# Eight loads for the edge rows and a new order at the start of a pooling and ConvFFN layer

## Chip, cores and metric

The kernel runs on one core of one Trainium2 chip (trn2). The metric is device time in microseconds (us) of one execution. The engines are called PE (TensorE; PEld is its weight load), ACT (ScalarE), DVE (VectorE), POOL (GpSimd) and SP (SyncE, which here only issues transfers).

## What is computed

One decoder layer in float32, x of 1024 positions by 1024 features: a norm, a causal pooling over windows of 2, 4, 8 and 16 positions (each for a quarter of the features) minus the position itself, a 256 x 256 product per quarter, a residual; then a second norm and a gated ConvFFN with 2816 hidden features.

```python
h = rms_norm(x, norm_mix_g)
# per group: mean of the last w positions of h, minus h; product with pool_w; bias; scale
x = x + pool_scale * (einsum('bsgc,gcd->bsgd', d, pool_w) + pool_b)
f = rms_norm(x, norm_ffn_g)
h = causal_depthwise_conv(f @ ffn_w_in, ffn_conv_w, ffn_conv_b)    # 3 taps
val, gate = split(h, 2)
out = x + (silu(gate) * val) @ ffn_w_out
```

## The kernel before

The layer has two parts. The large one (from 59 us on) is the ConvFFN: both products run on PE as seven-product block schemes (`step`, L384, and the output loop up to L723) over float32 operands split in a high and a low half. The change does not touch it. The small one, the mixer, runs over eight tiles of 128 positions, and the change is in the order of its first three tiles (L457 to L488) and in what is loaded ahead of them (L90 to L146).

For tile j the mixer works so. `load_x` (L85) brings x of the tile into SBUF. `stat(j)` (L453) squares and sums it on ACT (`rstd_of`, L155), takes the root there and three small steps on DVE, which give the factor of the norm. `mixer_norm(j)` (L174) multiplies a constant band matrix by that factor on DVE (`bandr`), so that the norm and the pooling are one product: `mixer_window(j)` (L234) multiplies x by the band on PE into a PSUM tile `psd`, adds the rows of the tile before (the edges) on DVE and copies the result to `dh` on ACT. `mixer_out(j)` (L254) multiplies `dh` by the pooling weights `wps` into `psy`, adds the bias rows by a product with ones (L262), adds x on DVE (L265) and stores the sum to DRAM (L266). `mixer_out_stats`, `ffn_norm` and `ffn_operand` then do the second norm and transpose the tile for the ConvFFN.

Ahead of that, things are made once: the weights `wps` (L205, eight DVE steps: pool_w times the pooling scale spread over partitions by `scale_rows`, times the norm's gain per partition from `par_sb`); the bias rows (`pool_bias`, L214, in two halves, loaded SBUF to SBUF into `bias_hl`); the second norm's factors spread over the partitions (`gain_spread` and `gain_rows`); and the edges: the last 16 positions of all eight tiles in one tile `x_edge` (L142), squared and normed as a tile of its own (`edge_norm`, L171) and multiplied by an edge band (`mixer_edges`, L187). `first_edges` (L246) adds the edges to tile 1's `dh`, which `mixer_window(1)` has already copied.

The order on each engine is written out: `with tc.issue_after(marks[...])` holds an instruction's place in the program behind a marked one, and each engine works strictly in its order. PE also has idle products (`keep_warm`, L127), whose result nobody reads. SP issues the loads in the order in which they are written. Every transfer of SP or ACT takes the next of eight semaphores in turn, and before a semaphore is taken again its last transfer must have landed.

## Time and profile before

| what | us |
|---|---|
| median of the runs | 703.62 |
| lowest run | 703.33 |
| profiled execution, its own time | 702.61 |
| span of its instructions | 700.9 |
| PE busy | 693.9 |
| DVE busy | 600.5 |
| ACT busy | 343.2 |
| POOL busy | 12.5 |

The profile is that of one execution. The span goes from the first to the last instruction; the execution's own time has 1.7 us more around it. Matmuls overlap in PE, so a row's length there is from the start of the first to the end of the last, and the next row can start before. On ACT and DVE too the next instruction may start some 0.1 us before the one before it ends.

### The profile page before, as it was taken

To read this page: it belongs to the slowest core of one execution; us is meant where nothing else is said; L and a number is where in the kernel's file an instruction comes from. 1 tells how busy PE (TensorE), PEld (TensorE's weight loads), DVE (VectorE), ACT (ScalarE), POOL (GpSimd) and SP (SyncE) were. 2 spreads that over 40 slices of the span, in tenths; PEclk is the share of its full clock that TensorE was granted. 3 is DMA by queue.
4 is the path that set the end of the run, shared out by engine and by line. 5 is a ranking of instruction groups with operands and counts; after the bars stand their busy time and mean duration, and the time that the engine had idled before them with its cause. 6 is when DMAs were issued, how large, how long until landed. Compare 5 with 4: busy or idle time off the path is not lost.

```text
span 700.9 us, 8493 instructions
## 1 busy us (share of the span) xinstructions
PE 693.9 (99%) x3154; PEld 573.7 (82%) x3154; DVE 600.5 (86%) x885; ACT 343.2 (49%) x515; POOL 12.5 (2%) x30
## 2 busy tenths in 40 slices
PE   8999999999999999999999999999999999999998
PEld 5898778888888888888888888888888888888886
DVE  5688999999888888888988888876887988999985
ACT  4786545454444444444545454454554444444431
POOL 3110000000000000000000000000000000000000
PEclk9999999999999999999999999999999999999999
DMA  9854112232222112222222212229989700122131
GB/s 307 302 141 121 57 65 91 89 122 91 67 84 74 60 78 90 91 90 91 91 90 91 86 65 91 91 84 338 335 305 335 277 22 1 61 90 87 64 106 60
DMA packets 32555, 85.47 MB, mean 122 GB/s; under 512 B 3689, under 2 KB 5377, under 8 KB 29698
## 3 DMA queue, kind: packets, MB, share of 16 engines
q1 hardware_dynamic: 31296, 82.82, 32.8%
q0 software_dynamic: 1184, 2.11, 1.8%
q8 instruction: 24, 0.39, 0.2%
q14 instruction: 17, 0.14, 0.1%
q10 hardware_dynamic: 34, 0.01, 0.0%
HBM read 62.89 MB, written 19.92 MB: 118 GB/s over the span
## 4 chain that ended last, share of the span: by engine, by line
PE 96%; DVE 2%; DMA 1%; ACT 1%; issue 0%; ACTq 0%; DVEq 0%
PE oP L723 30%; PE Y L372 26%; PE Z L372 17%; PE X L372 16%; PE psy L259 3%; PE psd L180 2%; DMA bias_hl<-rows_raw 1%; PE pst L292 1%; PE psy L262 1%; DVE n2f L323 0%; DMA x<-in_x_dram 0%; DVE T L312 0%; PE ps_edges L180 0%; PE ps_gain L227 0%; DVE n L277 0%; DVE S4s L77 0%
## 5 line engine op out<-in xcount | busy, mean ns | idle before, releaser
L723 PE MATMUL oP<-oBP,oAP 128*128 128x512 f32 (+1 forms) x924 | 208.8, 388 | 0.0
L723 PEld LDWEIGHTS oP<-oBP,oAP 128*128 128x128 f32 x924 | 172.9, 188 | 36.0 <-DVE oBP L77 0.3
L372 PE MATMUL Z<-T,S1s 128*128 128x512 f32 x264 | 64.0, 390 | 1.4 <-ACT T L311 1.2
L372 PE MATMUL X<-B,A11s 128*128 128x512 f32 x264 | 64.3, 390 | 0.0
L372 PE MATMUL Y<-T,S2s 128*128 128x512 f32 x264 | 64.0, 390 | 0.0
L372 PE MATMUL X<-B,A12s 128*128 128x512 f32 x264 | 63.5, 389 | 0.0
L372 PE MATMUL Y<-T,S3s 128*128 128x512 f32 x264 | 63.4, 389 | 0.0
L372 PE MATMUL Y<-T,A22s 128*128 128x512 f32 x264 | 63.4, 389 | 0.0
L372 PE MATMUL Z<-B,S4s 128*128 128x512 f32 x264 | 63.2, 389 | 0.0
L372 PEld LDWEIGHTS Z<-T,S1s 128*128 128x128 f32 x264 | 49.3, 188 | 12.6 <-ACT T L311 1.6
L372 PEld LDWEIGHTS Y<-T,S2s 128*128 128x128 f32 x264 | 49.4, 188 | 10.8 <-ACT S2s L76 0.4
L372 PEld LDWEIGHTS Y<-T,S3s 128*128 128x128 f32 x264 | 49.5, 188 | 10.3
L372 PEld LDWEIGHTS Z<-B,S4s 128*128 128x128 f32 x264 | 49.5, 188 | 10.3
L372 PEld LDWEIGHTS Y<-T,A22s 128*128 128x128 f32 x264 | 49.5, 188 | 10.3
L372 PEld LDWEIGHTS X<-B,A12s 128*128 128x128 f32 x264 | 49.5, 188 | 10.2
L372 PEld LDWEIGHTS X<-B,A11s 128*128 128x128 f32 x264 | 49.4, 188 | 10.2
L76 ACT ACTIVATE oBP<-blk 128x512 fp32r<-128x512 f32 x53 | 33.5, 633 | 49.1 <-PE oP L723 32.2
L77 DVE TENSOR_TENSOR oBP<-blk,oBP 128x512 fp32r<-128x512 f32 x53 | 36.6, 691 | 13.3 <-ACT oBP L76 13.3
L430 ACT ACTIVATE gate<-gate 128x1024 f32<-128x1024 f32 x22 | 23.3, 1061 | 44.5 <-DVE gate L421 44.5
L76 ACT ACTIVATE oAP<-blk 128x512 fp32r<-128x512 f32 x55 | 34.1, 621 | 19.2 <-DVE blk L323 15.9
L326 DVE TENSOR_TENSOR win<-win 128x512 f32<-128x512 f32 x60 | 41.3, 688 | 1.1
L77 DVE TENSOR_TENSOR oAP<-blk,oAP 128x512 fp32r<-128x512 f32 x55 | 37.7, 685 | 2.6 <-ACT oAP L76 2.6
(128 smaller groups left out, 941.4 us busy)
## 6 DMA issues: line engine op xcount, KB each, us to landing
win<-in_w_in_dram SPq DMA_DIRECT2D x22, 1024.0 KB, 4.8
g_dram<-val SPq DMA_DIRECT2D x22, 512.0 KB, 2.7
blk<-g_dram SPq DMA_DIRECT2D x33, 256.0 KB, 5.4
blk<-in_w_out_dram SPq DMA_DIRECT2D x31, 256.0 KB, 5.6
A12s<-g_dram SPq DMA_DIRECT2D x22, 256.0 KB, 5.3
B21s<-in_w_out_dram SPq DMA_DIRECT2D x22, 256.0 KB, 2.6
x<-in_x_dram SPq DMA_DIRECT2D x8, 512.0 KB, 7.0
x_dram<-x SPq DMA_DIRECT2D x8, 512.0 KB, 2.6
```

Of the source, the lines that this page charges most:

```text
L76: nc.scalar.activation(t[:, 0, :], src, AF.Copy)
L77: m = nc.vector.tensor_tensor(t[:, 1, :], src, t[:, 0, :].bitcast(F32), ALU.subtract)
L180: m = nc.tensor.matmul(ps[:, c * P : (c + 1) * P], src[:, c * P : (c + 1) * P], weights[:, c // 2, :], start=True, stop=True)
L259: nc.tensor.matmul(o, dh[:, c, :], wps[:, c, :], start=c % 4 == 0, stop=False, skip_group_check=True)
L262: m = nc.tensor.matmul(ps[:, cols], ones, bias_hl[:, cols], start=False, stop=True, skip_group_check=True)
L292: nc.tensor.transpose(ps[:, c * P : (c + 1) * P], n2[:, c * P : (c + 1) * P], ident)
L326: nc.vector.tensor_tensor(out, a, b, ALU.add)
L372: nc.tensor.matmul(bank, a[:, i, ks], b[:, l, k, :], start=opens and m == 0, stop=m == 11, skip_group_check=not opens)
L430: nc.scalar.activation(gate, gate, AF.Silu)
L723: nc.tensor.matmul(bank, a[:, u, i * P : (i + 1) * P], b[:, v, c], start=opens and first, stop=g == NP2 - 1 and m == 2, skip_group_check=n ...
```

## The change

What it does: the edge rows come by eight loads of 16 rows each in place of one load with rows 128 apart. The memset under the pooling scale's row is shared between DVE and POOL, and ACT issues the row's load ahead of its table load. The second norm's factors are spread on PE by eight products whose stationary operand is one column of `par_sb` repeated 128 times and whose moving operand is the identity, in place of a DVE step and two wide products with ones. Three of the eight weights and tile 1's averages are placed ahead of tile 0's window work on DVE, the other five behind tile 1's band. One of the eight idle products at the start and the five later ones go. The small loads are put in another order, and the bias rows' two loads go from ACT's queue to SP's, ahead of x3 to x7. mixer_out(0) goes behind mixer_window(1).

PE, from tile 0's weights to tile 1's. `psdJ` is tile J's window, `psyJ` its product with the weights and the bias rows, `ps_gain` the second norm's factors, `ps_edges` the edges, `idle` an idle product. Before:

```order
L130 LDWEIGHTS idle_87
L130 MATMUL idle_ps_123<-idle_87 128x512
L259 MATMUL psy0_239<-wps_159,dh0_214 128x256 x8
L262 MATMUL psy0_239<-bias_hl_95,ones_156 128x512 x2
L180 MATMUL psd1_252<-bandr1_236,x1_137 128x128 x8
L227 MATMUL ps_gain_263<-spread_155,ones_156 128x512 x2
L180 MATMUL ps_edges_276<-edge_band_84,x_edge_83 128x128 x8
L180 MATMUL psd2_322<-bandr2_294,x2_142 128x128 x8
L259 MATMUL psy1_334<-wps_159,dh1_261 128x256 x8
L262 MATMUL psy1_334<-bias_hl_95,ones_156 128x512 x2
```

After, from the scale rows on:

```order
L197 MATMUL ps_scale0_182<-rows_raw_85,ones_151 128x512
L197 MATMUL ps_scale1_183<-rows_raw_85,ones_151 128x512
L178 MATMUL psd0_221<-bandr0_193,x0_132 128x128 x8
L223 MATMUL ps_gain_248<-cst_81,par_sb_122 128x128 x8
L178 MATMUL psd1_259<-bandr1_233,x1_136 128x128 x8
L255 MATMUL psy0_270<-wps_154,dh0_230 128x256 x8
L258 MATMUL psy0_270<-bias_hl_96,ones_151 128x512 x2
L178 MATMUL ps_edges_283<-edge_band_84,x_edge_83 128x128 x8
L178 MATMUL psd2_329<-bandr2_301,x2_149 128x128 x8
L255 MATMUL psy1_341<-wps_154,dh1_268 128x256 x8
L258 MATMUL psy1_341<-bias_hl_96,ones_151 128x512 x2
```

The factors and tile 1's window now stand ahead of tile 0's product with the weights, and no idle product is left behind the scale rows; the edges and tile 2's window follow as before.

DVE, from the last of the steps for tile 0 to the edges. `x0<-psy0` is the addition of x for tile 0, `st_e` and `edge_band` belong to the edge rows' norm, `st_a2` and `bandr2` to tile 2's, `st_b0` to tile 0's second norm, `dh1` takes the edges. Before:

```order
L212 TENSOR_TENSOR spread_155<-cst_81,par_sb_121 128x1024
L265 TENSOR_TENSOR x0_132<-psy0_239,x0_132 128x1024
L160 TENSOR_SCALAR st_e_269<-st_e_269 128x1
L162 SCALAR_TENSOR_TENSOR st_e_269<-st_e_269 128x1
L163 RECIPROCAL st_e_269<-st_e_269 128x1
L167 TENSOR_SCALAR edge_band_84<-cst_81,st_e_269 128x512
L160 TENSOR_SCALAR st_a2_288<-st_a2_288 128x1
L162 SCALAR_TENSOR_TENSOR st_a2_288<-st_a2_288 128x1
L163 RECIPROCAL st_a2_288<-st_a2_288 128x1
L167 TENSOR_SCALAR bandr2_294<-band_82,st_a2_288 128x512
L160 TENSOR_SCALAR st_b0_297<-st_b0_297 128x1
```

After:

```order
L202 SCALAR_TENSOR_TENSOR wps_154<-ps_scale1_183,par_sb_122,wp_raw_123 128x256 x4
L158 TENSOR_SCALAR st_e_241<-st_e_241 128x1
L160 SCALAR_TENSOR_TENSOR st_e_241<-st_e_241 128x1
L161 RECIPROCAL st_e_241<-st_e_241 128x1
L165 TENSOR_SCALAR edge_band_84<-cst_81,st_e_241 128x512
L158 TENSOR_SCALAR st_a2_295<-st_a2_295 128x1
L160 SCALAR_TENSOR_TENSOR st_a2_295<-st_a2_295 128x1
L161 RECIPROCAL st_a2_295<-st_a2_295 128x1
L165 TENSOR_SCALAR bandr2_301<-band_82,st_a2_295 128x512
L261 TENSOR_TENSOR x0_132<-psy0_270,x0_132 128x1024
L158 TENSOR_SCALAR st_b0_304<-st_b0_304 128x1
L245 TENSOR_TENSOR dh1_268<-ps_edges_283,dh1_268 128x8x16
```

The addition of x0 has moved from ahead of the edge rows' and tile 2's averages to behind both; the spread is gone; the edges are added to dh1 behind the first step of tile 0's second norm, where three steps of it stood ahead (L249).

SP, the loads from the first to x3 or x4. `cst` are the constants, `par_sb` columns of parameters, `wp_raw` the halves of the pooling weights. Before:

```order
L90 DMA x0_132<-in_x_dram 128x1024
L134 DMA cst_81<-in_consts_dram 128x384
L135 DMA par_sb_121<-in_par_dram 128x16
L137 DMA wp_raw_122<-in_pool_w_dram 128x4x256
L90 DMA x1_137<-in_x_dram 128x1024
L137 DMA wp_raw_122<-in_pool_w_dram 128x4x256
L140 DMA cst_81<-in_consts_dram 128x384
L142 DMA x_edge_83<-in_x_dram 128x1x1024
L90 DMA x2_142<-in_x_dram 128x1024
L90 DMA x3_144<-in_x_dram 128x1024
L90 DMA x4_146<-in_x_dram 128x1024
```

After:

```order
L90 DMA x0_132<-in_x_dram 128x1024
L134 DMA cst_81<-in_consts_dram 128x384
L136 DMA wp_raw_123<-in_pool_w_dram 128x4x256
L90 DMA x1_136<-in_x_dram 128x1024
L139 DMA cst_81<-in_consts_dram 128x384
L140 DMA par_sb_122<-in_par_dram 128x16
L136 DMA wp_raw_123<-in_pool_w_dram 128x4x256
L143 DMA x_edge_83<-in_x_dram 16x1024 x8
L90 DMA x2_149<-in_x_dram 128x1024
L213 DMA bias_hl_96<-rows_raw_85 1x8x128 x2
L90 DMA x3_200<-in_x_dram 128x1024
L90 DMA x4_202<-in_x_dram 128x1024
```

The second part of the constants and the par columns now stand between x1 and the second half of the weights; the edge rows are eight loads; the bias rows' loads (before on ACT's queue) stand behind x2.

```diff
--- before.py
+++ after.py
@@ -100,17 +100,17 @@
     scale = rows_raw[:, 0, :]
     rows8, bias8 = (rows_raw[:NK, 1, i * NH : i * NH + 2 * P].rearrange("k (r p) -> k r p", p=P) for i in range(2))
     bias8 = bias8.bitcast(F32R)
-
-    nc.gpsimd.dma_start(rows8, rows.rearrange("r (k p) -> k r p", p=P))
     idle = work.tile([P, NH], BF16, tag="sum", name="idle", bufs=3)
     nc.vector.memset(idle, 0.0)
     eps_t = const.tile([P, 1], F32, tag="eps", name="eps_t")
     nc.vector.memset(eps_t, D * EPS)
+    nc.vector.memset(scale[:, :NH], 0.0)
+    nc.gpsimd.memset(scale[:, NH:], 0.0)
     warm = pp.tile([P, 1], F32, tag="warm", name="warm")
-    table = nc.scalar.activation(warm, eps_t, AF.Sqrt).ins
-    nc.vector.memset(scale, 0.0)
-    with tc.issue_after(table):
-        nc.scalar.dma_start(scale[:1, :], rows[:1, :])
+    with tc.issue_after(nc.scalar.dma_start(scale[:1, :], rows[:1, :]).ins):
+        nc.scalar.activation(warm, eps_t, AF.Sqrt)
+
+    nc.gpsimd.dma_start(rows8, rows.rearrange("r (k p) -> k r p", p=P))
     bias_hl = pp.tile([P, D], F32R, tag="bias_hl", name="bias_hl")
     nc.gpsimd.memset(bias_hl.bitcast(F32), 0.0)
     for g, w in enumerate(WINDOWS):
@@ -123,27 +123,25 @@
     par_sb = const.tile([P, NPAR], F32, tag="par", name="par_sb")
     wp_raw = raw_tile("wp_raw").rearrange("p a (c d) -> p (a c) d", d=GRP)
 
-    idle_ps = ps_x.tile([P, NH], F32, tag="X", name="idle_ps")
+    idle_ps = bank2("idle_ps")[:, :NH]
 
     def keep_warm(n):
         for _ in range(n):
             nc.tensor.matmul(idle_ps, idle[:, :P], idle, start=True, stop=True)
 
-    keep_warm(8)
+    keep_warm(7)
     load_x(0)
     nc.sync.dma_start(cst[:, :E0], consts[:, :E0])
-    nc.sync.dma_start(par_sb[:, GM:], par[:, GM:])
     for g in range(0, NG, 2):
         nc.sync.dma_start(wp_raw[:, 2 * g : 2 * g + 4, :], pool_w[g : g + 2].rearrange("g (k p) d -> p (g k) d", p=P))
         if g == 0:
             load_x(1)
-    nc.sync.dma_start(cst[:, E0:], consts[:, E0:])
-
-    nc.sync.dma_start(x_edge, x.rearrange("(j r) d -> r j d", r=P)[P - HALO :, :, :])
-    for j in range(2, NS):
-        load_x(j)
-    nc.sync.dma_start(par_sb[:, :GM], par[:, :GM])
-    spread = hls.tile([P, NK, P], F32, tag="hl", name="spread", bufs=7)
+            nc.sync.dma_start(cst[:, E0:], consts[:, E0:])
+            nc.sync.dma_start(par_sb[:, GM:], par[:, GM:])
+
+    for j in range(NS):
+        nc.sync.dma_start(x_edge[j * HALO : (j + 1) * HALO, :], x[(j + 1) * P - HALO : (j + 1) * P, :])
+    load_x(2)
 
     band0 = cst[:, :FAC].bitcast(BF16).rearrange("p (g s) -> p g s", s=P)
     fac = cst[:, FAC:E0].rearrange("p (c t) -> p c t", t=HALO)
@@ -194,37 +192,35 @@
     wps = pp.tile([P, 2 * NG, GRP], F32, tag="wps", name="wps")
     def scale_rows():
 
-        ps = bank2("ps_scale")
+        ps = [ps_x.tile([P, NH], F32, tag="X", name=f"ps_scale{h}") for h in range(2)]
         for h in range(2):
-            cols = slice(h * NH, (h + 1) * NH)
-            marks["scale"] = nc.tensor.matmul(ps[:, cols], ones.bitcast(F32), scale[:, cols], start=True, stop=True).ins
-        return ps
+            marks["scale"] = nc.tensor.matmul(ps[h], ones.bitcast(F32), scale[:, h * NH : (h + 1) * NH], start=True, stop=True).ins
+        return [ps[g // 2][:, g % 2 * GRP : (g % 2 + 1) * GRP] for g in range(NG)]
 
     def mixer_weights(scale_b, chunks):
         for c in chunks:
             marks["wps"] = nc.vector.scalar_tensor_tensor(
-                wps[:, c, :], scale_b[:, c // 2 * GRP : (c // 2 + 1) * GRP], par_sb[:, GM + c : GM + c + 1], wp_raw[:, c, :], op0=ALU.mult, op1=ALU.mult
+                wps[:, c, :], scale_b[c // 2], par_sb[:, GM + c : GM + c + 1], wp_raw[:, c, :], op0=ALU.mult, op1=ALU.mult
             ).ins
 
-
-    def gain_spread():
-        gain = par_sb[:, GF : GF + NK].unsqueeze(2).to_broadcast([P, NK, P])
-        marks["spread"] = nc.vector.tensor_tensor(spread, ident[:, None, :].to_broadcast([P, NK, P]), gain, ALU.mult).ins
 
     def pool_bias():
         b8 = rows8[:, 1, :]
         nc.vector.tensor_tensor(b8, b8, rows8[:, 0, :], ALU.mult)
         marks["bias"] = nc.scalar.activation(bias8[:, 0, :], b8, AF.Copy).ins
-        nc.vector.tensor_tensor(bias8[:, 1, :], b8, bias8[:, 0, :].bitcast(F32), ALU.subtract)
+        marks["bias_dve"] = nc.vector.tensor_tensor(bias8[:, 1, :], b8, bias8[:, 0, :].bitcast(F32), ALU.subtract).ins
         for l in range(2):
-            nc.scalar.dma_start(bias_hl[l : l + 1, :].bitcast(F32), bias8[:, l, :].bitcast(F32))
+            m = nc.sync.dma_start(bias_hl[l : l + 1, :].bitcast(F32), bias8[:, l, :].bitcast(F32)).ins
+        with tc.issue_after(m):
+            for j in range(3, NS):
+                load_x(j)
+            nc.sync.dma_start(par_sb[:, :GM], par[:, :GM])
 
     def gain_rows():
         ps = bank2("ps_gain")
-        flat = spread.rearrange("p k s -> p (k s)")
-        for h in range(2):
-            cols = slice(h * NH, (h + 1) * NH)
-            marks["gain_pe"] = nc.tensor.matmul(ps[:, cols], ones.bitcast(F32), flat[:, cols], start=True, stop=True).ins
+        for k in range(NK):
+            gain = par_sb[:, GF + k : GF + k + 1].to_broadcast([P, P])
+            marks["gain_pe"] = nc.tensor.matmul(ps[:, k * P : (k + 1) * P], gain, ident, start=True, stop=True).ins
         gain_b = pp.tile([P, D], F32, tag="gain_b", name="gain_b")
         marks["gain"] = nc.scalar.activation(gain_b, ps, AF.Copy, scale=FOLD).ins
         return gain_b
@@ -459,29 +455,26 @@
     mixer_norm(0)
     with tc.issue_after(marks["band0"]):
         pool_bias()
-    with tc.issue_after(marks["scale"]):
-        keep_warm(1)
+    with tc.issue_after(marks["bias"]), tc.issue_after(marks["bias_dve"]):
+        mixer_weights(scale_b, range(3))
+        stat(1)
+    with tc.issue_after(marks["scale"]), tc.issue_after(marks["wps"]), tc.issue_after(marks["a1"]):
         mixer_window(0)
-    with tc.issue_after(marks["psd0"]):
-        keep_warm(4)
     with tc.issue_after(marks["first"]):
-        mixer_weights(scale_b, range(2 * NG))
-    with tc.issue_after(marks["dh0"]), tc.issue_after(marks["wps"]):
-        stat(1)
         mixer_norm(1)
     with tc.issue_after(marks["band1"]):
-        gain_spread()
-    with tc.issue_after(marks["spread"]):
+        mixer_weights(scale_b, range(3, 2 * NG))
+    with tc.issue_after(marks["dh0"]), tc.issue_after(marks["wps"]):
+        edge_norm()
+    with tc.issue_after(marks["psd0"]), tc.issue_after(marks["e"]):
+        gains.append(gain_rows())
+    with tc.issue_after(marks["gain_pe"]), tc.issue_after(marks["gain"]):
+        mixer_window(1)
+    with tc.issue_after(marks["psd1"]):
         mixer_out(0, stats=False)
     with tc.issue_after(marks["psy0"]):
-        mixer_window(1)
-    with tc.issue_after(marks["psd1"]):
-        gains.append(gain_rows())
-    with tc.issue_after(marks["a1"]), tc.issue_after(marks[0]):
-        edge_norm()
-    with tc.issue_after(marks["gain_pe"]):
         mixer_edges()
-    with tc.issue_after(marks["e"]), tc.issue_after(marks["edge"]):
+    with tc.issue_after(marks["dh1"]), tc.issue_after(marks["edge"]):
         stat(2)
         mixer_norm(2)
     with tc.issue_after(marks["a2"]), tc.issue_after(marks["band2"]):
@@ -761,7 +754,7 @@
     inside = [(r > t - w) & (r <= t) for w in WINDOWS]
     first = [(m - np.eye(P) * np.minimum(t + 1, w)) / w * FOLD for m, w in zip(inside, WINDOWS)]
 
-    row, src, dst = r // NS, r % NS, t // HALO
+    src, row, dst = r // HALO, r % HALO, t // HALO
     edge = [((src + 1 == dst) & (row - HALO > t % HALO - w)) / w * FOLD for w in WINDOWS]
 
     def packed(blocks):
```

## Rows read from the trace of the kernel before

**Rows 1.** The page, part 1 (busy time of each engine, its share of the span, instructions) and, of part 2, the clock granted to TensorE in 40 equal slices of the span, in tenths:
```profile
PE 693.9 (99%) x3154; PEld 573.7 (82%) x3154; DVE 600.5 (86%) x885; ACT 343.2 (49%) x515; POOL 12.5 (2%) x30
...
PEclk9999999999999999999999999999999999999999
```

**Rows 2.** The timeline of the first 30 us, PE's rows: start in us, length in us, engine, line, operation, tiles, count, and in brackets the idle time before it with what ended it:
```profile
1.26 3.59 PE L130 MATMUL idle_ps<-idle 128*128 128x512 bf16 x8 [1.26 <-DVE eps_t L108]
...
4.99 2.62 PE L200 MATMUL ps_scale<-rows_raw,ones 128*128 128x512 f32 x4
...
7.66 1.95 PE L180 MATMUL psd<-bandr,x 128*128 128x128 f32 x16
...
9.44 1.03 PE L130 MATMUL idle_ps<-idle 128*128 128x512 bf16 x4
...
11.05 3.72 PE L259 MATMUL psy<-wps,dh 128*128 128x256 f32 x16 [0.58 <-ACT dh L244]
...
14.94 0.70 PE L262 MATMUL psy<-bias_hl,ones 128*128 128x512 f32 x2 [0.17 <-DMA bias_hl<-rows_raw]
...
22.55 3.62 PE L259 MATMUL psy<-wps,dh 128*128 128x256 f32 x16
...
26.47 1.95 PE L180 MATMUL psd<-bandr,x 128*128 128x128 f32 x16
```

**Rows 3.** The chain of waits that ended last, in order of time, from 8 to 21 us: start in us, length in us, what:
```profile
8.37 6.49 DMA bias_hl<-rows_raw
...
15.64 1.78 PE psd L180 x16
17.43 1.72 PE ps_gain L227 x4
```

**Rows 4.** The timeline from 58 to 100 us: the first product with w_in on PE, and DVE's addition of the last tiles:
```profile
59.41 3.00 PE L372 MATMUL X<-B,A11s 128*128 128x512 f32 x12
...
66.37 1.22 DVE L265 TENSOR_TENSOR x<-psy,x 128x1024 f32<-128x1024 f32 x1 [1.42 <-PE psy L262]
```

**Rows 5.** The timeline of the first 30 us, the start of ACT and DVE (ACTq is a DMA issued by ACT):
```profile
0.80 1.28 ACT L110 ACT_TABLE_LOAD   x1 [0.80 <-PEq L799]
...
1.37 0.91 DVE L111 MEMSET rows_raw<- 128x1024 f32 x1 [0.16 <-issue]
...
2.10 0.20 ACT L110 ACTIVATE warm<-eps_t 128x1 f32<-128x1 f32 x1
...
2.32 0.51 ACTq L113 DMA_DIRECT2D rows_raw<-in_rows_dram  x1
...
4.05 1.06 ACT L158 ACTIVATE junk_a<-x 128x1024 bf16<-128x1024 f32 x1 [1.75 <-DMA x<-in_x_dram]
```

**Rows 6.** The same timeline, ACT and DVE from 9 to 26 us:
```profile
9.85 3.22 DVE L205 SCALAR_TENSOR_TENSOR wps<-ps_scale,par_sb,wp_raw 128x256 f32<-128x256 f32 x8
9.98 1.02 ACT L244 ACTIVATE dh<-psd 128x1024 f32<-128x1024 f32 x1 [2.54 <-DVE psd L241]
...
13.12 1.06 ACT L158 ACTIVATE junk_e<-x_edge 128x1024 bf16<-128x1024 f32 x1 [0.75 <-DMA x_edge<-in_x_dram]
...
14.50 1.04 ACT L158 ACTIVATE junk_a<-x 128x1024 bf16<-128x1024 f32 x1
...
15.66 0.30 ACT L159 ACTIVATE st_a<-st_a,eps_t 128x1 f32<-128x1 f32 x1
15.68 1.23 DVE L265 TENSOR_TENSOR x<-psy,x 128x1024 f32<-128x1024 f32 x1 [0.31 <-PE psy L262]
...
19.42 1.01 ACT L229 ACTIVATE gain_b<-ps_gain 128x1024 f32<-128x1024 f32 x1
...
21.18 0.27 DVE L249 TENSOR_TENSOR dh<-ps_edges,dh 128x128 f32<-128x128 f32 x1
...
24.67 0.15 DVE L160 TENSOR_SCALAR st_a<-st_a 128x1 f32<-128x1 f32 x1 [1.54 <-ACT st_a L159]
...
25.31 0.55 DVE L167 TENSOR_SCALAR bandr<-band,st_a 128x512 f32<-128x512 f32 x1
```

**Rows 7.** DMA. For x0 and the two halves of the pooling weights, the issue on SP (how long it took in ns, its start in us) and the time from issue to landing; what SP's queue waited for until 60 us (us in total, times, longest); and three windows: stretch, busy us of PE, PEld, DVE, ACT, POOL with counts, then granted clock, DMA share, GB/s:
```profile
L90 SPq DMA_DIRECT2D x<-in_x_dram x1: 383/383/383, 0.8 to 0.8; - x1
...
DMA to landing us min/median/max: 3.2/3.2/3.2
L137 SPq DMA_DIRECT2D wp_raw<-in_pool_w_dram x1: 434/434/434, 2.2 to 2.2; - x1
...
DMA to landing us min/median/max: 4.3/4.3/4.3
L137 SPq DMA_DIRECT2D wp_raw<-in_pool_w_dram x1: 433/433/433, 3.2 to 3.2; - x1
...
DMA to landing us min/median/max: 6.7/6.7/6.7
SPq L90 <- DMA wp_raw<-in_pool_w_dram: 2.1, 2, 1.5
...
5.00:10.00 5.00, 5.00 (x24) 3.34 (x25) 2.07 (x8) 0.82 (x5) 1.96 (x8) 1.00 1.08 349
...
10.50:11.00 0.50, 0.00 (x0) 0.00 (x0) 0.50 (x2) 0.50 (x2) 0.00 (x0) 1.00 1.07 262
...
16.00:16.50 0.50, 0.50 (x7) 0.50 (x7) 0.50 (x1) 0.00 (x0) 0.00 (x0) 1.00 1.00 401
```

## Prediction

> **What bounds the kernel now.** I read the page first. PE is busy for 693.9 of 700.9 us, and the granted clock stands at nine tenths or more in every slice [rows 1], 1.00 in each window of [rows 7]: a gain can only be time in which PE stands, or works for nothing. So I looked next where PE is not at useful work in the stretch that the change touches, the first 27 us, in the timeline of PE [rows 2]. Eight idle products fill it until 4.9. They take 0.45 us each and the four later ones 0.26 each, at the same granted clock: 512 columns in 0.43 us is the 1.2 GHz level, and half of that the 2.4 GHz level, which PE reached while it worked through the fillers and the first scale product. The scale rows run from 4.99 to 7.6, the first window (psd0) starts at 7.66. Then come four idle products (1.03 us), 0.58 us of waiting for dh0 and 0.17 us of waiting for the bias rows. From 14.94 on PE has no gap: the chain of waits holds nothing but PE from there [rows 3]. Useless in all: about 0.4 (the eighth filler), 0.2 (the one filler ahead of psd0), 1.03, 0.58 and 0.17, some 2.4 us. That is the most that this change can give, 0.3% of the run. A shift of PE by a us or two lives to the end: at 66.4 DVE waited 1.42 us for PE just before it took up the long series of sums that bounds the stretch after it [rows 4], so that series moves with PE.
>
> **The change part by part.** The sum is made against the profiled execution's own 702.6 us (its span 700.9 and 1.7 around it). The median of the runs shown, 703.6, stands 1.0 above it.
>
> *Scale row sooner.* DVE's memset of the row (0.91 us) is halved with POOL, so ACT issues the load at about 1.9 and not 2.32. Its 0.51 us now stands ahead of the table load (1.28) and the warm-up activation (0.2): 1.9 + 0.51 + 1.28 + 0.2 = 3.9, and the square of x0 starts at 4.05 when x0 lands [rows 5]. Cost nothing, with 0.15 to spare; if the memset on POOL is late, some tenths at psd0, which is not on the path that decides (below). POOL's own load, of the rows cut in eight, starts some 0.5 later; what is made of it, the bias rows, PE needs at 16.
>
> *Fillers.* Seven, then none: the scale products start at about 4.5, psd0 at about 7.05, 0.6 sooner. A window takes 1.78 [rows 3]. The norm's factors are now sixteen passes of 128 columns, as a window has, so 1.78 for the 1.72 before [rows 3]; DVE's spread goes. They stand right behind psd0: 8.85 to 10.6.
>
> *Three weights and tile 1's averages ahead.* Their par load now stands behind x1 in the queue. It lands between the two halves of the weights, that is between 2.2 + 4.3 = 6.5 and 3.2 + 6.7 = 9.9 [rows 7]; I take 8.4. Three weights at 0.40 (eight take 3.22) then end at 9.6, DVE's correction of psd0 stands behind them, and dh0 starts at 10.0, as it does at 9.98 now [rows 6]. Nothing won, nothing lost; with the far bound dh0 is 1.4 later, which the edge load below covers. ACT no longer issues the two bias loads (SP does), so it squares x1 as soon as it has landed, and tile 1's bands are there at about 11.0. psd1 runs 11.0 to 12.8, psy0 and its bias (3.7 and 0.5) to 16.8, where before they ended at 15.6 but without psd1 and the factors: PE is ahead by 1.78 + 1.72 - 1.2 = 2.3 us there.
>
> *The edge rows.* Before, one load with scattered rows: DMA moved 262 GB/s in 10.5 to 11.0 and 401 at 16.0 [rows 7], and ACT waited until 13.12 for it [rows 6]. Now eight loads of 64 KB each. The queue waits for landings: SP stood 2.1 us on the two weight loads [rows 7], as every load takes its semaphore from the eighth before it. By that count the eighth edge load waits for the second half of the weights. This landed at 9.9; a further 192 KB (the constants) now stands ahead of it, at 349 GB/s [rows 7] 0.55 us: 10.45. How long a 64 KB load takes the trace does not show. x0, 512 KB into an empty queue, took 3.2 from issue to landing [rows 7], of which 1.3 to 1.5 are bytes at 349 to 401 GB/s; so 1.8 and 0.2 for 64 KB, 2.0, an estimate from these rows. The edge rows land at 12.45. Bounds: ACT is not free for them before dh0 has left it at 11.0 (E = 11.0); and if a load takes what the first half of the weights took in a filled queue, 4.3, they land at 14.8; by the second half's 6.7 at 17.2. I take 12.45, since by then the queue has little left.
>
> *What follows from the edge rows.* From here on ACT and DVE, not PE, set the pace, in the new order. With E the start of the edge square on ACT: square, sum and root 1.38 (13.12 to the next at 14.50), the factors' copy and dh1 at 0.92 each (1.01 long, the next starts 0.1 before the end), square and root of x2 1.46 (14.50 to 15.96) [rows 6]: E + 4.68 = 17.1. DVE's four small steps to tile 2's bands take 1.19 (24.67 to 25.86): 18.35. Only now comes the addition of x0 (1.22): 19.55, where it ran at 15.68 before [rows 6]; it has been moved behind two averages. ACT's square and root of the result take 1.46, one small DVE step 0.15: the edge addition to dh1 starts at 21.15. Before it started at 21.18 [rows 6]. So PE, which has psd2 done by 20.5, waits for it and starts psy1 at 21.45 and not at 22.55. From the edge addition to tile 3's bands the order of ACT and DVE is all but the same, 4.68 us (21.18 to 25.86), with one DVE step moved by 0.15: bands at 26.0. PE is through with psy1 at 21.45 + 3.5 + 0.5 = 25.4 and waits. psd3 starts at 26.0, before at 26.47 [rows 2]. That is the sum: 2.3 us ahead at the edge windows, 1.1 at psy1, 0.5 at psd3, and from there PE has its inputs early again. 702.6 - 0.5 = 702.1; the median stands 1.0 higher: 703.1.
>
> *What else moves.* The bias loads stand behind x2 on SP's queue; PE needs them at 16.3. Issued at about 11.5, they have 4.8 us; on ACT's queue the second took 6.49 to be there [rows 3]. With that, psy0 ends 1.7 later, DVE's addition of x0 0.4 to 0.9 later, and the gain is gone. SP's store of x0 now stands ahead of the first w_in load, and that of x1 ahead of the next three, which go out some 10 us later than now; the first product with them starts at 59.4 [rows 4], so I count nothing.
>
> **The rivals.** *Edge rows in time (faster).* If the last of the eight is not held up and lands by 11.0, every step after E moves with it: 1.45 us more, so about -1.9, near the ceiling of 2.4: 700.7, as a median 701.7. For it: the bytes are no more than before and no longer scattered. Against: the semaphore count above.
>
> *Edge rows late (slower).* The loads touch 16 partitions each and queue behind each other; each that waits holds up x2 and the bias rows behind it on SP. If the last takes 4.3 us, as the first half of the weights did, E = 14.8, and all of the chain comes 2.35 later: psd3 at 28.35, 1.9 after now: 704.5, median 705.5. It decides from E = 12.9 on, where psd3 is at 26.47 again. For it: the weight loads took 4.3 and 6.7 [rows 7]. Against: both were queued behind 512 KB loads, which are done by then.
> The Trainium skill has a rule on this side (SBUF — State Buffer, Door 1: The DMA port swizzle): how fast a transfer runs depends on how many of SBUF's 16 ports its partitions reach, and partitions 0..15 reach four, measured there at 104 GB/s. By that page eight loads of 64 KB take 0.63 us each, 5.0 in all, an estimate: from 9.5 on they land near 15, the slower rival's time. No run shown here has a load of 16 partitions.
>
> *The clock.* Five fillers inside the stretch are gone. If PE falls back to 1.2 GHz for as long as it stood there at the start, some 4 us, 2 us of work are added, of which 1.1 fall into PE's new waits: +0.4 against now, 703.0, median 704.0. Against: the gaps that I find are 1 us at most, and the factors and psd1 fill the place of the fillers.
>
> **How the numbers follow.** Forecast (E between 12 and 13) 0.50; edge rows in time 0.18; edge rows late 0.24; clock 0.05; none of these 0.03. The range goes from the faster rival to a little beyond the slower one's 705.5: 701.6 to 705.9. The forecast's own: 702.7 to 703.7. A change of 2% (14 us), about what a measurement of this kernel can tell from no change, is out of reach of every case: the ceiling of the gain is 2.4 us, and for a loss of 14 PE would have to stand as long as the whole stretch lasts. So faster 0.01, same 0.97, slower 0.02.
>
> **What would show it.** In the profile after: the edge square's start on ACT at 12 to 13, released by the edge load; psd0 near 7.1, no PE gap over 0.5 us before the edge windows; then a PE wait of about 1 us ahead of psy1, ended by DVE's edge addition, and one of about 0.6 ahead of psd3, ended by DVE's bands. Wrong, if psd3 starts before 25 (the chain through ACT is not what sets it) or after 27, if PE waits for the bias rows, or if the start of psd3 differs from now by another amount than the end of the run does (the shift is not carried).

## The result: slower by a third of a per cent

| | before | after |
|---|---|---|
| median of 9 runs (us) | 703.33 | 705.81 |
| ratio, 95% interval | | 1.0036 [1.0024, 1.0048] |
| profiled execution, its own time | 702.61 | 706.61 |
| its span | 700.9 | 704.5 |

One of before's nine executions took 790.45 and is not in the ratio. The forecast was a median of 703.1, 0.5 below the 703.6 that stood for before; the time rose by 2.5 us, within what was called no change at 2%. It lies where the rival "edge rows late" put it (705.5).

PE in the first 32 us after (start, length, idle time before it with what ended it), to be read against [rows 2, 3]:

```profile
4.60 2.12 PE L197 MATMUL ps_scale<-rows_raw,ones 128*128 128x512 f32 x4 [0.17 <-DMA rows_raw<-in_rows_dram]
6.88 2.05 PE L178 MATMUL psd<-bandr,x 128*128 128x128 f32 x16 [0.17 <-DVE bandr L165]
11.25 3.29 PE L223 MATMUL ps_gain<-cst,par_sb 128*128 128x128 f32 x16 [2.31 <-DMA par_sb<-in_par_dram]
14.33 2.36 PE L178 MATMUL psd<-bandr,x 128*128 128x128 f32 x16
16.52 3.62 PE L255 MATMUL psy<-wps,dh 128*128 128x256 f32 x16
...
24.75 3.72 PE L255 MATMUL psy<-wps,dh 128*128 128x256 f32 x16 [0.58 <-DVE dh L245]
...
29.31 2.02 PE L178 MATMUL psd<-bandr,x 128*128 128x128 f32 x16 [0.37 <-ACT junk_a L156]
```

psd0 is 0.8 sooner, and then PE stands for 2.31 us, until the second part of the constants (10.91) and the par columns (11.12) have landed; the factors need both. psd3 starts at 29.31, before at 26.47 [rows 2]: 2.84 later. ACT and DVE in the same stretch, against [rows 5, 6]:

```profile
4.13 1.06 ACT L156 ACTIVATE junk_a<-x 128x1024 bf16<-128x1024 f32 x1 [0.25 <-DMA x<-in_x_dram]
...
10.13 1.06 ACT L156 ACTIVATE junk_a<-x 128x1024 bf16<-128x1024 f32 x1 [1.62 <-DMA x<-in_x_dram]
...
11.24 1.27 DVE L202 SCALAR_TENSOR_TENSOR wps<-ps_scale,par_sb,wp_raw 128x256 f32<-128x256 f32 x3 [2.42 <-DMA x_edge<-in_x_dram]
...
12.80 1.02 ACT L240 ACTIVATE dh<-psd 128x1024 f32<-128x1024 f32 x1 [1.20 <-DVE psd L237]
...
15.78 1.06 ACT L156 ACTIVATE junk_e<-x_edge 128x1024 bf16<-128x1024 f32 x1 [1.95 <-DMA bias_hl<-rows_raw]
...
24.41 0.28 DVE L245 TENSOR_TENSOR dh<-ps_edges,dh 128x128 f32<-128x128 f32 x1
...
28.66 0.55 DVE L165 TENSOR_SCALAR bandr<-band,st_a 128x512 f32<-128x512 f32 x1
```

What a load starts now waits for it: x1's square (x1 landed at 10.11, before at 8.07), the three weights, dh0 (12.80 against 9.98) and the edge square, which starts at 15.78 as the last edge load lands (15.68). Two of the waits are put down to a later load on the same semaphore: the weights waited for the par columns (landed 11.12), the edge square for the eighth edge load. The chain of waits that ended last, in order of time (start, length, what), says which load holds it:

```profile
3.70 9.93 DMA wp_raw<-in_pool_w_dram
13.63 0.01 issue
13.65 0.31 SPq L143
13.96 0.04 issue
14.00 0.42 SPq L90
...
15.78 1.16 ACT junk_e L156 x2
```

The second half of the weights, issued at 3.70, lands at 13.63; 0.02 later SP issues the eighth edge load (L143), then x2. Three windows (stretch, busy us of PE, PEld, DVE, ACT, POOL, granted clock, DMA share, GB/s), against [rows 7]:

```profile
5.00:10.00 5.00, 3.77 (x20) 2.27 (x19) 1.64 (x6) 0.89 (x4) 1.98 (x9) 1.00 1.00 317
8.00:12.00 4.00, 1.69 (x15) 1.53 (x14) 1.21 (x4) 1.75 (x4) 0.00 (x0) 0.97 0.80 240
12.00:16.00 4.00, 4.00 (x24) 4.00 (x24) 3.56 (x12) 1.24 (x2) 0.00 (x0) 0.60 0.47 138
```

From 12 to 16 DMA moves only 138 GB/s: twelve of the 16 DMA engines were through with the seventh edge load at 13.45, and the eighth went out at 13.65, when the last engine had brought the weights. After PE stood from 8.94 to 11.25 its granted clock is 0.60 from 12 to 16, mostly the 1.2 GHz level: from the start of the factors to that of psd1 it takes 3.08 and not 1.78. The shift goes on to the ConvFFN, whose first product started at 59.41 before [rows 4]:

```profile
62.44 3.01 PE L368 MATMUL X<-B,A11s 128*128 128x512 f32 x12
```

That is 3.03 later, and the span is 3.6 longer.

### The profile page after: what moved, and what is told of

Read it like the earlier page. It is cut to its first block, busy times and chain, and to the rows that moved or that the text cites. A ratio compares the mean times of both kernels' runs of the same rounds, so it can differ in the third digit from the quotient of the medians.

```text
span 704.5 us, 8517 instructions
## 1 busy us (share of the span) xinstructions
PE 694.3 (99%) x3160; PEld 575.5 (82%) x3160; DVE 598.8 (85%) x884; ACT 343.4 (49%) x515; POOL 13.1 (2%) x31
## 4 chain that ended last, share of the span: by engine, by line
PE 94%; ACT 2%; DVE 2%; DMA 2%; SPq 0%; issue 0%; DVEq 0%; ACTq 0%
PE oP L716 30%; PE Y L368 26%; PE Z L368 17%; PE X L368 16%; PE psy L255 3%; DMA wp_raw<-in_pool_w_dram 1%; PE psd L178 1%; PE pst L288 1%; DVE n2f L319 0%; ACT junk_a L156 0%; PE psy L258 0%; ACT junk_b L156 0%; DVE T L308 0%; ACT dh L240 0%; SPq L90 0%
```

## The experiments

Below, "before" is the run beside each group (703.4 to 703.8). "Low clock" counts the executions whose mean granted clock was 0.998 or less; of before there was none among 125.

| run | what differs | median | ratio to before, 95% | low clock |
|---|---|---|---|---|
| e1 | after, again | 705.58 | 1.0030 [1.0019, 1.0040] | 3 of 12 |
| e2 | after, one edge load | 703.76 | 1.0004 [0.9995, 1.0012] | 1 of 11 |
| e3 | before, eight edge loads | 706.05 | 1.0037 [1.0023, 1.0052] | 8 of 12 |
| e4 | after, old order of small loads | 705.53 | 1.0036 [1.0021, 1.0050] | 8 of 11 |
| e5 | after, idle products | 705.83 | 1.0028 [1.0016, 1.0040] | 0 of 6 |
| e6 | e4, idle products | 704.57 | 1.0014 [1.0003, 1.0024] | 1 of 11 |
| e7 | after, two edge loads, tiles outside | 710.91 | 1.0104 [1.0088, 1.0119] | 4 of 4 |
| e8 | one edge load early, tiles outside | 709.63 | 1.0088 [1.0074, 1.0103] | 5 of 5 |
| e9 | before, again (one execution) | 703.13 | | 0 of 1 |
| e10 | e8, rows outside | 706.48 | 1.0035 [1.0023, 1.0047] | 11 of 12 |
| e11 | after, two edge loads, rows outside | 704.22 | 1.0009 [1.0000, 1.0018] | 0 of 11 |
| e12 | after, one edge load, old order | 704.24 | 1.0011 [0.9997, 1.0025] | 7 of 12 |
| f1 | after, dh1's edges ahead on DVE | 705.76 | 1.0031 [1.0019, 1.0043] | 2 of 5 |
| f2 | e12, idle products | 703.63 | 1.0008 [0.9995, 1.0022] | 3 of 12 |
| f4 | before, five idle products less | 703.84 | 1.0004 [0.9996, 1.0013] | 0 of 11 |
| f5 | e12, identity early | 703.25 | 0.9998 [0.9990, 1.0007] | 1 of 12 |
| g1 | before, scale row sooner | 703.53 | 1.0001 [0.9989, 1.0013] | 0 of 12 |
| g2 | f5, again (one execution) | 702.64 | | 0 of 1 |

### Which loads: e1 to e4

> The changed kernel once more, unchanged, for a second profile of its start. In its first profile the first half of the pooling weights landed at 8.5 us (6.5 in the kernel before), three or four of the 16 DMA engines having fallen behind between 4.1 and 6.6 us (packets of 1 KB up to 0.8 us long), and everything behind it in the queue landed 2 to 3.7 us late; the edge square started at 15.8. Theory A (the order of the loads or their shape causes it): the same again, first weights at 8 to 9 us, edge square at 15 to 16, time 705.8 +- 0.7. Theory B (an accident of that one execution): first weights at 6.5 us, edge square below 14, and then the loss of 2.5 us has another cause, since the median of nine runs has it.

e2, and the reverse in e3 (each with the order of the edge band's rows to match):

```diff
-    for j in range(NS):
-        nc.sync.dma_start(x_edge[j * HALO : (j + 1) * HALO, :], x[(j + 1) * P - HALO : (j + 1) * P, :])
+    nc.sync.dma_start(x_edge, x.rearrange("(j r) d -> r j d", r=P)[P - HALO :, :, :])
```

> The changed kernel with the edge rows by one load of scattered rows (as before), all else as changed. Theory A1 (the eight loads of 16 partitions cost the time, by what they do to the queue ahead of and among them): first weights land at 6.5, second at about 10.5, edge square at about 13.1, and the time falls to 703.4. Theory A2 (the par columns and constants ahead of the second half of the weights, or another thing of the new order): first weights stay at 8.5, edge square at 15 or later, time 705.5 to 706.

> The kernel before with only the edge load replaced by the eight loads. Theory A1 (the eight loads cost the time): the second half of the weights lands later than 9.95, the edge square starts at 15 or later instead of 13.1, time 705 to 706. Theory A2 (the order of the small loads): weights at 6.5 and 10 as before, edge square at 12.5 to 13.5, time 703 to 703.6.

e4: `par_sb` behind the first `cst`, the second `cst` behind both halves of the weights, as before.

> The changed kernel with its eight edge loads, but the small loads in the order of the kernel before: the par columns ahead of the first half of the weights, the second part of the constants behind the second half. Theory A1 (eight loads): weights and edge rows late as in the changed kernel, edge square at 15 to 16, time 705.5 to 706. Theory A2 (order of the small loads): par at 5.3, second half of the weights at 10, edge square at 12.5 to 13.5, time 702.8 to 703.5.

By time, one load takes back 1.8 of the loss, and eight loads alone in the kernel before cost 2.5; the old order of the small loads does nothing. But the profiles do not show it as theory A1 had it. Edge square and psd3 in e1, e4 and e2 (e2 also with the edge addition to dh1):

```profile
14.22 1.06 ACT L156 ACTIVATE junk_e<-x_edge 128x1024 bf16<-128x1024 f32 x1 [2.04 <-DMA bias_hl<-rows_raw]
...
27.75 2.02 PE L178 MATMUL psd<-bandr,x 128*128 128x128 f32 x16 [0.37 <-ACT junk_a L156]
```

```profile
13.69 1.06 ACT L156 ACTIVATE junk_e<-x_edge 128x1024 bf16<-128x1024 f32 x1 [2.33 <-DMA bias_hl<-rows_raw]
...
27.22 2.02 PE L178 MATMUL psd<-bandr,x 128*128 128x128 f32 x16 [0.32 <-ACT junk_a L156]
```

```profile
14.47 1.06 ACT L155 ACTIVATE junk_e<-x_edge 128x1024 bf16<-128x1024 f32 x1 [2.15 <-DMA x_edge<-in_x_dram]
...
21.41 0.28 DVE L244 TENSOR_TENSOR dh<-ps_edges,dh 128x128 f32<-128x128 f32 x1
...
27.22 2.02 PE L177 MATMUL psd<-bandr,x 128*128 128x128 f32 x16 [0.82 <-ACT junk_a L155]
```

With eight loads psd3 stands 13.53 behind the edge square each time (14.22 to 27.75, 13.69 to 27.22, after 15.78 to 29.31). With one load the edge rows land no sooner (14.45), but psd3 follows after 12.75: the edit also changed the order that the scheduler wrote, and dh1's edges stand ahead of the first step of tile 0's second norm on DVE, not behind it. So e2 is two edits in one.

How much the order is worth the profiles tell. X, the first product of the ConvFFN, starts 46.66 to 46.68 behind the edge square in after, e1 and e4 (15.78 to 62.44, 14.22 to 60.90, 13.69 to 60.35), whatever the loads did, and 45.65 to 45.72 in e2, e7, e11, e12, f5 and g2, with one or two loads. (In e8 and e10 PE's wait for the identity comes between, in f2 idle products.) So about 1.0 of e2's 1.8 goes with the order on ACT and DVE and not with the landing of the rows.

e3 is two edits in one too. Its rows landed late, at 15.63 (13.09 in before): the sixth load went out at 12.70, as the first of the bias rows' loads had landed (12.69). But the scheduler also put the copy of dh1 ahead of the edge square on ACT, which then started at 20.35, 4.7 after its rows had landed; PE stood 2.03 ahead of the edges and had a clock of 0.58 from 24 to 28. What e3 shows of eight loads by themselves is the late landing, not its price.

### The clock, and the number of loads: e5 to e8

e5 and e6 put eight idle products ahead of the factors and four ahead of psy1:

```diff
         ps = bank2("ps_gain")
+        keep_warm(8, ps[:, :NH])
```

> The changed kernel with eight idle products ahead of the factors' products and four ahead of psy1, where PE waits. They cost nothing where PE would stand anyway, some 2 us at the first place (before psd1, which is ahead of need) where it would not. Theory C (half of the loss is the clock: where PE stands over 2 us ahead of the factors, it is granted 1.2 GHz for some 4 us and the rest of the start is late): no execution with a mean granted clock under 0.999, the spread of the times narrows to within 1.5 us, median 704.3 to 705.0. Theory D (only the late edge rows, through ACT and DVE, count; the clock's fall lies under that wait): median 705.3 to 706 and a spread of 3 us as in the changed kernel.

> The kernel with eight edge loads and the old order of the small loads (median 705.5, its executions at a granted clock of 1.000 at 703.5 to 704.0, those at 0.994 to 0.998 at 705 to 708), with the same twelve idle products. Theory C (clock): all executions near 704, median 703.6 to 704.3, none above 705.5. Theory D (waits alone): median 705 to 706, spread as without the idle products.

The low clock goes in e5, and the spread with it (704.6 to 706.4), but the median stays (six executions): in the changed kernel the clock falls under a wait that is there anyway, and makes the upper tail alone (e1's three at 705.9 to 708.2). That is theory D, but for the spread. In e6 the median falls by 1.0 (the ratio from 1.0036 to 1.0014; the intervals overlap a little), to 704.57, between the two theories, and one execution stays at 707.2. In e4 the executions at 1.000 took 703.5 to 704.0, those below 705 to 708. So there the clock carries part of the loss; how much of it is the late load that makes PE stand, and not the clock, is not shown. In e4's own profile PE stood 2.40 and the clock held.

> The changed kernel with the edge rows by two loads of 64 partitions (each four blocks of 16 rows), all else as changed. Neither has to wait for the second half of the weights to land, as the eighth of eight did. Theory A3 (the number of loads, of which the last waits for the weights, costs the time): edge rows land about 1 us behind the weights and not 2, x2 goes out at 6 us, median 703.5 to 704.3. Theory A4 (blocks of rows next to each other in DRAM, however loaded, slow the queue): as the changed kernel, 705.3 to 706.

> The changed kernel with the par columns early, as before, and the edge rows by one load ahead of the second part of the constants and the second half of the weights. By the chain of the prediction (13.5 us from the edge square to psd3 and the shift carried to the end) the edge rows land at 10 to 11, the edge square stands right behind dh0 at 11 to 11.5, psd3 at 24.5 to 25, the time 701.3 to 702.2, faster than before. The rival: the second half of the weights now lands at 12 to 13, the last weights end at 14 to 14.5, psy0 and the addition of x0 are 1 to 2 us later and take the place of the edge rows: psd3 at 26 to 27, 703 to 704.

Both told nothing on their question. A load of four blocks of 16 rows, with the tiles as the outer dimension, was carried by four of the 16 DMA engines: in e7 twelve engines were through with x2 at 14.2 and four at 21.3 to 22.4; in e8, with eight tiles outside, eight engines were late (the edge rows landed at 16.02). In e8 PE stood 7.15 us for the constants behind that load:

```profile
16.44 3.73 PE L222 MATMUL ps_gain<-cst,par_sb 128*128 128x128 f32 x16 [7.15 <-DMA cst<-in_consts_dram]
```

The Trainium skill states this (DMA: Bandwidth & Descriptors, Why a DMA increments its semaphore by 16 and not by 1): the number of engines is the largest up to 16 that divides the slowest dimension of both sides. The two runs agree with it, with four and eight.

### The same with the load spread: e9 to e12

> The kernel before, unchanged, for a second profile of its loads. If the late engines belong to the new kernels alone, the first half of the weights lands at 6.5 to 6.8 us again and no packet before 5.5 takes over 0.4 us; if they are an accident that any execution can have, it lands at 7 us or later here too, and the edge square starts up to 1 us later than 13.1 without more than 0.5 us of it in the time.

> The changed kernel with par early and the edge rows by one load ahead of the constants' second part and the second half of the weights, now with the 16 rows as the outer dimension of the load, as before (the run with the eight tiles outside put the load on eight of the 16 DMA engines). By the chain of the prediction: edge rows land at 10 to 11, edge square at 11 to 11.8, psd3 at 24 to 25, time 701.3 to 702.5. Rival: the second half of the weights comes at 12 to 13 and holds psy0 and the addition of x0; 703 to 704.

> The changed kernel with the edge rows by two loads of 64 partitions, 16 rows outside and four tiles inside, so that each is spread over all 16 DMA engines. Theory A3 (the wait of the eighth load for the weights, then 2 us, is what costs): as with one load, 703.5 to 704.2, edge rows about 2 us behind the weights' last engine or less, no granted clock under 0.998. Theory A5 (any load with rows next to each other, or more loads, disturbs the queue): 705 to 706.

> The changed kernel with the loads of the kernel before (edge rows by one load, par early, the constants' second part behind the weights); what is left of the change is the sooner scale row, the factors by PE, the dropped fillers and the order on the engines. The edge rows land at 13.1 to 14. Theory E (the loads are the whole loss, the rest of the change is worth its small gain): 702.6 to 703.4. Theory F (the rest costs too: without the fillers the clock falls, or the factors wait for the identity, which lands with the constants' second part): 703.8 to 705, some executions with a granted clock under 0.999.

e9 moved the ground: the late engines are in the kernel before too. Its first weights landed at 7.19 (6.53 in the first profile), the second half at 10.67, and the edge square started at 13.78:

```profile
13.78 1.06 ACT L158 ACTIVATE junk_e<-x_edge 128x1024 bf16<-128x1024 f32 x1 [1.32 <-DMA x_edge<-in_x_dram]
...
15.36 0.69 PE L262 MATMUL psy<-bias_hl,ones 128*128 128x512 f32 x2 [0.49 <-DMA bias_hl<-rows_raw]
...
15.89 1.95 PE L180 MATMUL psd<-bandr,x 128*128 128x128 f32 x16
...
26.89 1.95 PE L180 MATMUL psd<-bandr,x 128*128 128x128 f32 x16
```

In the first profile psd1 started so:

```profile
15.48 1.95 PE L180 MATMUL psd<-bandr,x 128*128 128x128 f32 x16
```

The edge square is 0.66 later, psd3 0.42 and the time 0.5, but the edge rows did not cost it. PE waited 0.49 for the bias rows (0.17 in the first profile), which made psd1 0.41 later, and from there it had no gap: psd3 stands 10.99 to 11.00 behind psd1 in before, e9, f4 and g1, with the edge square at 13.12 to 14.09. In before's order edge rows up to there cost nothing.

In the profiles with the edge rows behind the weights and spread over all engines, without e3, the last edge row lands 6.2 to 7.7 us behind the last engine of the first weights, in 15 of 16 between 6.2 and 7.2, with one, two or eight loads; in e3, where a load waited for the bias rows, 8.5. What differs is when the first weights are there: 6.5 to 7.2 in the three profiles with the old start of the program (before, e9, f4), 6.9 to 9.0 in thirteen with the new start.

In e11 two loads did about as well as one, at the edge of theory A3's range by time, but not for A3's reason: the edge rows landed 2.0 behind the weights there, as in the changed kernel (13.83 and 15.87), and no sooner; its order is that of one load, 45.65 from the edge square to X. e10's edge rows landed at 13.39 and not at 10 to 11, the chain's gain did not come, and PE stood 4.82 for the identity, which now lay behind them; in 11 of 12 executions the clock fell. In e12 it stood for the same reason:

```profile
12.25 2.02 PE L222 MATMUL ps_gain<-cst,par_sb 128*128 128x128 f32 x16 [3.08 <-DMA cst<-in_consts_dram]
```

Its five executions from 702.96 to 703.76 had a clock of 0.999 or 1.000, the seven with less took 704.2 to 707.0.

### Order, fillers, and useful work in the gap: f1 to f5

f1 holds the small steps of tile 0's second norm on DVE:

```diff
+        with ExitStack() as late:
+            if name == "b0":
+                late.enter_context(tc.issue_after(marks["dh1+"]))
+            nc.vector.tensor_scalar(st[:, 0:1], st[:, 0:1], D * EPS, None, op0=ALU.add)
```

> The changed kernel, loads as changed, with one difference in order: on DVE the edge addition to dh1 stands ahead of the first small step of tile 0's second norm and not behind it (in the changed kernel that step waits for ACT's square of the new x0, and the addition behind it for nothing else). Theory G (this order is one term of the loss: 13.5 us from the edge square to psd3, 12.75 in the profiles with one or two edge loads, where the addition stands first): psd3 12.0 to 12.8 us behind the edge square, median 0.7 to 1.3 below the changed kernel's 705.7: 704.4 to 705.0. Theory H (only the loads count): 705.4 to 706.

```profile
15.65 1.06 ACT L156 ACTIVATE junk_e<-x_edge 128x1024 bf16<-128x1024 f32 x1 [2.29 <-DMA x_edge<-in_x_dram]
...
27.79 2.02 PE L181 MATMUL psd<-bandr,x 128*128 128x128 f32 x16 [0.20 <-issue]
...
36.89 3.29 PE L258 MATMUL psy<-wps,dh 128*128 128x256 f32 x14 [0.49 <-DVE x L264]
```

The chain is 12.14 long, as theory G said, and the time is not lower: part is given back two tiles later, where PE now waits 0.49 for DVE, and X starts at 62.00, 46.35 behind the edge square. This is not e2's order: there DVE also adds the edges to psd2 ahead of the last steps of tile 0's second norm, and in f1 ACT copies dh2 behind one square more. So f1 tests a part of that order, and wins at X a third of e2's 1.0.

> The kernel with one edge load and the old order of the small loads (executions at a granted clock of about 1.000 at 703.0, the others, 0.995 to 0.998, at 704.2 to 707.0), with eight idle products ahead of the factors' products, where PE stood from 9.2 to 12.3 waiting for the identity. Theory C (PE's standing there brings the clock down in half of the executions): none under 0.999, median 702.8 to 703.4, none above 704.5. Theory D (the waits, not the clock): median 704.2 as without.

> The kernel before without its five later idle products (one ahead of psd0, four behind it), nothing else. PE then stands from about 9.2 to 11.05, some 1.9 us. Theory C (a PE that stands brings the clock down): some executions with a granted clock of 0.998 or less, median 704 to 705. The other case (1.9 us of standing is too little): all at 0.999 or 1.000, median 703.3 to 703.6, since nothing waits for these products.

f2 lowers e12's median by 0.6, but the intervals of the two overlap, and three executions of 12 stay at 0.997 (706.3 to 706.7): the eight products end at 10.9, and PE still stood 2.43 in the profile. In f4 it stood 1.45, and no execution had a low clock; so the five later fillers of before cost or save nothing that was measured.

f5 loads the identity behind the par columns:

```diff
+    nc.sync.dma_start(cst[:, ID:], consts[:, ID:])
...
-    nc.sync.dma_start(cst[:, E0:], consts[:, E0:])
+    nc.sync.dma_start(cst[:, E0:ID], consts[:, E0:ID])
```

> The kernel with one edge load and the old order of the small loads, and the identity (64 KB of the constants) loaded right behind the par columns, so that the factors can run at 9.2 and fill PE's gap with useful work. Theory C: no granted clock under 0.999, median 702.6 to 703.2 (the edge rows at 13.1 to 14.4 still set psd3 at 26 to 27). Rival: the gap comes back ahead of psd1 or psy0, and the clock falls in some executions: 703.5 to 704.5.

```profile
8.81 1.95 PE L223 MATMUL ps_gain<-cst,par_sb 128*128 128x128 f32 x16
12.08 2.02 PE L178 MATMUL psd<-bandr,x 128*128 128x128 f32 x16 [1.32 <-issue]
...
27.36 2.02 PE L178 MATMUL psd<-bandr,x 128*128 128x128 f32 x16 [0.82 <-ACT junk_a L156]
```

The factors fill the gap as the prediction wanted, the clock holds in 11 of 12, and the kernel is as fast as before (703.25, just above theory C's 702.6 to 703.2). No version beat the kernel before by more than its interval.

### Whether the sooner scale row makes the loads late: g1, g2

> The kernel before with one part of the change alone: the row's memset shared between DVE and POOL and the scale row issued ahead of the table load. Theory I (this part makes the engines of the queue fall behind at 4 to 6 us: the first half of the weights landed at 6.5 to 7.2 in five profiles with the old block and at 6.8 to 9.5 in thirteen with the new one): first weights at 7.5 or later, edge square at 14 or later, median 704.0 to 704.8. Theory J (the lateness comes from elsewhere or is chance): first weights at 6.5 to 7.2, median 703.2 to 703.6, since psd0's sooner start is followed by idle products and wins nothing.

> The kernel with one edge load, the old order of the small loads and the identity early, once more, for a second profile beside the run of the kernel before with the scale row sooner. First weights at 7.5 to 8.5 as in its first profile under theory I, edge square at 14 to 15, time 702.2 to 704.9 as its twelve executions.

(g2's label names a later scale row; the kernel is that of f5.) g1's first weights landed at 7.44, between the theories, and its edge square started at 14.09, in theory I's range; its time is that of before, in theory J's. In that order psd3 then starts at 26.95: PE, which stood 1.29 for the bias rows, sets it, and not the edge rows. So the sooner scale row costs nothing there, and whether it delays the loads stays open. g2's weights landed at 7.24 and its edge square started at 13.43, both sooner than expected; the time was 702.64. (The expectation counts five and thirteen profiles; the traces here have four with the old start, at 6.5 to 7.2, and fourteen with the new, at 6.8 to 9.5, ahead of g1 and g2.)

## Why the prediction was wrong, step by step

**Scale row, fillers, psd0: right.** ACT issued the row at 1.84, x0's square started at 4.13 (4.05 before), psd0 at 6.88 (forecast 7.05).

**The par columns: mis-sized.** Forecast 8.4, bounds 6.5 to 9.9; they landed at 11.12 (9.47 in e1). The factors also need the identity, in the second part of the constants, which the prediction put at nothing: it landed at 10.91. With these loads the three weights, dh0 (12.80 for 10.0) and the factors (11.25 for 8.85) were late, so PE was not 2.3 us ahead at the edge windows but 1.5 behind (20.44, before 18.98). The 2.3 has a slip of its own: 12.8 + 3.7 + 0.5 is 17.0 and not 16.8, which gives 2.1.

**The step that failed: "The edge rows land at 12.45."** Its form was right in two terms. The eighth load does wait for the second half of the weights (landed 13.63, issued 13.65; in e1 12.13 and 12.15), and takes 2.0 from there (15.68; 14.12). The third was wrong: the weights' landing, set at 10.45 from 9.95 of one execution plus 0.55, was 11.7 to 13.8 in the seven profiles with the new order (after, e1, e2, e5, e7, e11, f1). In before's program, the constants behind it, it was 9.8 to 11.1 (before, e9, f4, g1). And the check by bytes was missing. Up to the last edge row both kernels load the same 2952 KB through the same queue, and before had them at 13.1, 13.8 and 13.6 (before, e9, f4), never at 12.45. Cutting the last load in eight moves no byte forward. By the prediction's own signs (the edge square at 12 to 13, psd3 not after 27) this step was wrong.

**The chain from the edge rows: right.** Forecast 13.55 to psd3 (26.0 − 12.45), measured 13.53 in four profiles (after, e1, e4, e5); one for one, since 1.56 later edge rows (e1 to after) are 1.56 at psd3. This is what makes the late rows dear: in before's order PE and not the edge rows set psd3, with the edge square at 13.12 to 14.09 (before, f4, e9, g1). From the edge square to X the changed kernel takes 46.67; X started at 59.41 to 59.91 in those four, so the edge square has to start by 12.7 to 13.2 to lose nothing, and it started at 15.78 and 14.22.

**The shift is carried: right in sign, short in size.** From psd3's 2.84 to 3.03 at X and 4.0 in the own time of the two profiled executions; the medians differ by 2.5. Of the last 1.0, 0.6 are in the span behind X and 0.4 around it; what they are is not shown.

**Rival "edge rows late": the outcome, not for its reason.** With the edge square at 15.78 its own working gives psd3 at 29.33 (28.35 + 0.98); it was 29.31. That 705.5 is so near to 705.8 is luck in part: the rival's E = 14.8 comes from a load that takes 4.3, and the eighth took 2.0 behind late weights. Nor did the loads cost time by touching 16 partitions. The first seven landed at 13.88, 14.05, 14.23, 14.42, 14.59, 14.76 and 14.94: 0.18 apart, which for eight would be 1.4 us, an estimate.
The Trainium skill's port rule (SBUF — State Buffer, Door 1: The DMA port swizzle) gave 5.0 us for the eight; this trace has 0.18 each and not 0.63, though with several loads under way at once.

**Rival "clock": underweighted.** It had 0.05 and +0.4. The fall came behind a wait that the prediction did not have (2.31 us for par). It makes the slowest executions of the changed kernel, and up to 1 us of the median in e4 (e6).

**Bias rows: no wait, as forecast, but because PE was late.** They landed at 17.30 and 17.47, behind the 16.3 at which the forecast needs them; psy0's last products started at 19.79.

What stays open: why some DMA engines fall behind between 4 and 6.6 us in nearly every profile (single packets of 1 KB took 0.4 to 1.5 us there in after, e1 to e3, e9 and e11), why more so in the kernels with the new start, and how the 0.8 of e2's 1.8 us that the order (1.0 at X, of it 0.78 at psd3) leaves divide between the clock's tail and the rest.

## What to carry to other kernels

Before a load's landing is put into a sum, count all the bytes ahead of it in its queue and take landings from several executions, since the last of 16 engines decides; and ask what slack stands behind it, for a change that makes every engine wait for that load turns its spread into time. An edit to loads can change the order on other engines where a scheduler writes it, so compare the order too before a time is put down to the load. A gap on PE in the place of idle products is best filled with work whose inputs are there, or kept filled.

## What the runs showed of the hardware

- The outer dimension of a transfer sets how many DMA engines carry it: 4 and 8 tiles outside were carried by 4 and 8 of 16. Two such loads cost 6.7 us more than two with 16 rows outside (710.9, e11 704.2), one at e8's place 3 more (709.6, e10 706.5).
- The last of the 16 engines decides when a load has landed, and it differs between profiles: the second half of the weights landed at 12.13 and 13.63 in two profiles of the changed kernel, with twelve engines done at 10.67 and 10.92.
- PE that stood came back at a lower clock in some executions only: 0.60 from 12 to 16 after 2.31 us in after, 0.50 from 12 to 16 after 4.82 in e10, 0.50 from 16 to 20 after 7.15 in e8; but 1.00 in the profiled executions of f4 (1.45 us), f2 (2.43) and e12 (3.08), though e12 had a low clock in seven of its 12 executions and f2 in three.
